# Raw weight slots handed out in order of release, the decay's logarithm issued earlier, and three kinds of attention operations on ScalarE

## The chip, the cores and the metric

The kernel runs on one core of a Trainium2 chip. The metric is the time of one execution on the device in microseconds, the median of several runs; lower is better. The core's engines appear below as PE (TensorE, matrix products), DVE (VectorE), ACT (ScalarE), POOL (GpSimd) and SP (SyncE, which here only issues transfers). Each engine takes its own instructions strictly in order; semaphores make one engine wait for another.

## The reference

One layer with two head groups. 16 learned tokens stand ahead of 512 positions (L = 528), the width is 2048, all in float32:

```python
xn = rmsnorm(h, g_pre)
p = xn @ w_in                       # q, k, v, z_gla, r, hc, gate_b, gate_c, z_conv
log_a = log_sigmoid(r @ w_gate_up + b_gate) / GATE_TAU
o = gla_chunked(q * DK**-0.5, k, v, log_a)      # 4 heads, key 128, value 256, chunks of 64
y_gla = rmsnorm(o, g_gla_out) * silu(z_gla)
y_conv = gate_b * causal_dwconv(gate_c * hc, w_conv) * silu(z_conv)
y = concat([y_gla, y_conv]) @ w_out
return h + rmsnorm(y, g_post)
```

The chunked attention takes the running sum of `log_a` inside a chunk, scales q and k by exponentials of it, forms masked scores, and carries a state of 128 x 256 from chunk to chunk.

## The kernel before

Every float32 product is made of three faster ones. An operand is split into a high half (`whi`, a rounding copy on ACT) and a low half (`wlo`, the raw value minus the high half, on DVE), and PE adds hi*hi, hi*lo and lo*hi.

**Pairs and products.** Two column tiles of the input projection (say `z2` and `z3`) form a `Pair`. A pair is computed by a Strassen-like scheme from its four weight blocks "11", "12", "21", "22" in seven products, in the order P5, P1, P6, P2, P3, P7, P4 (`ORDER`). One product is 24 matmuls of 128 x 128 against about 260 columns. Tile names tell the place: `z2z3P` is the PSUM result of any product of that pair. The third matmul of a product is the first that reads `wlo`. P2 is added into P1's PSUM bank after ACT has copied the bank away (`q`), and P3 into P5's bank after the copy `f`.

**Preparing a product.** `prepare` for a product does up to one add or subtraction of raw blocks on DVE (`raw<-raw`, lines 188 and 218), then the split (`whi` on ACT, line 123, and `wlo` on DVE, line 124). There are three buffers each of `whi` and `wlo`, and products are prepared two ahead of PE (`AHEAD = 2`). `away` takes results out of PSUM, and after each product some steps of the attention generators in `STAGE` run: `decay` (d), `gla_b` (t), `gla_c` (s), `gla_d` (o), `gla_e` (g), one head after the other, from `k1q1` to `b0s0`. A `yield` ends a step.

**Raw slots.** A raw block is 128 x 1024 floats, loaded by one transfer on SP's queue (line 204). Five slots exist, one pool tag with five buffers. Block "21" is last read by the add of P6, "12" by the split of P3, "11" by the split of P7, "22" by the split of P4. `prepare` asks for the next pair's blocks by name at P5, P6 and P4.

**The order.** A scheduler in the framework puts the recorded instructions into one order per engine while the program is built; the places that it chooses are fixed from then on.

**Order of the whole.** First eight plain tiles and the normalisation of x (to about 86 us), then the pairs z2z3, k1q1, v2v3, z4z5, k2q2, v4v5, z6z7, k3q3, v6v7, h0c0, b0s0 with the attention of the four heads between them, then 14 pairs of the convolution, then the output projection and the closing normalisation. `ini` is a pool of the first stage; when it closes, the pools `ev` (the copies `f`, `q`, `u`, `v`) and `gla` take its memory, and a new tile there waits for the last reader of the old tile that lay in the same place.

Of the kernel before, what the change touches and what calls it, by code (L numbers as in the profile page):

```python
# [9 lines left out]
F32 = mybir.dt.float32  # L10
# [35 lines left out]
def hymba_kernel(ctx, tc, xT, x, g_pre, w_r, w_t, w_up, b_gate, g_gla, w_conv, w_o, g_post, out):  # L46
# [29 lines left out]
    wup = const.tile([RU, H * P], F32R, name="wup")  # L76
    bg = const.tile([P, H], F32, name="bg")
    gg = const.tile([P, 2], F32, name="gg")
    wc = const.tile([P, 8, 3], F32, name="wc")
# [39 lines left out]
    def split(raw, shape, pool=None):  # L119
# [5 lines left out]
        return hi, lo  # L125

    def new_raw(shape=None):
        return wp.tile(shape or [P, NB, P], F32, tag="raw", name="raw", bufs=5)

# [12 lines left out]
    def load_gran(name, g):  # L142
        gran = new_gran()
        fill_gran(gran, w_t[TILE[name]], 8 * g, 8 * g + 8)
        return gran

# [43 lines left out]
    class Pair:  # L190
        def __init__(self, na, nb, c0, dst, done=None, stages=(), before=(), per=2):
            self.na, self.nb, self.c0, self.w, self.dst = na, nb, c0, XHALF - c0, dst
            self.done, self.stages, self.before, self.per = done, stages, before, per
            self.raw, self.sb = {}, {}
            for name in ORDER:
                line.append((self, name, name == ORDER[-1]))

        def load(self, b):

            if b not in self.raw:  # L200
                r = new_raw()
                g = NB * (b in ("12", "22"))
                i = TILE[self.na if b[0] == "1" else self.nb]
                nc.sync.dma_start(r, w_t[i][:, g:g + NB, :])
                self.raw[b] = r

        def prepare(self, name, nxt):
            for b in ("21", "22", "11", "12"):
                self.load(b)
            raw = self.raw  # L210
# [10 lines left out]
            two = split(raw[b], [P, NB, P])  # L221
            if nxt and name in ("P5", "P6", "P4"):
                nxt.load({"P5": "21", "P6": "22", "P4": "11"}[name])
                if name == "P4":
                    nxt.load("12")
            return two
# [26 lines left out]
        def away(self, name):  # L253
# [23 lines left out]
            else:  # L277
                self.put(self.dst_b[0], sb["v"], sb["P4"], ALU.subtract)

    def prepare_next():  # L280
        n = len(ready)
        p, name, last = line[n]
        after = [q for q, _, _ in line[n:n + 9] if q is not p]
        ready.append(p.prepare(name, after[0] if after else None))

# [63 lines left out]
    class Whole:  # L349
# [3 lines left out]
        def __init__(self):  # L353
            self.raw, self.pt = {}, None
            for g in range(8):
                line.append((self, g, g == 7))

        def load(self, g):
            g = {"21": 0, "22": 1, "11": 2, "12": 3}.get(g, g)
            if g not in self.raw:  # L360
                r = self.raw[g] = new_raw([P, 2, 2 * OW])
                for c in range(2):
                    nc.sync.dma_start(r[:, :, c * OW:(c + 1) * OW], w_o[c, :, 2 * g:2 * g + 2, :])

        def prepare(self, g, nxt):
            for n in range(min(8, g + 4)):
                self.load(n)
            two = split(self.raw[g], [P, 2, 2 * OW])
            if g < 4:
                self.load(g + 4)  # L370
            else:
                nxt.load(("12", "22", "11", "21")[g - 4])
            return two
# [35 lines left out]
    class Out:  # L409
# [3 lines left out]
        def __init__(self, c, g):  # L413
            self.c, self.g, self.raw = c, g, {}
            self.end = c == 3 and g == 1
            for n in (LORDER if self.end else OORDER):
                line.append((self, n, n == "P4"))

        def load(self, b):
            if b not in self.raw:  # L420
                r = self.raw[b] = new_raw([P, 4, OW])
                k0 = 8 * (b[0] == "2") + 4 * self.g
                nc.sync.dma_start(r, w_o[2 * self.c + (b[1] == "2"), :, k0:k0 + 4, :])

        def prepare(self, name, nxt):
            raw = self.raw
# [9 lines left out]
            two = split(raw[{"P7": "12", "P3": "22", "P2": "21"}.get(name, "11")], [P, 4, OW])  # L436
            if nxt and name in ("P1", "P7", "P3", "P4"):
                nxt.load({"P1": "12", "P7": "22", "P3": "11", "P4": "21"}[name])
            return two
# [181 lines left out]

    with tc.tile_pool(name="ini", bufs=1, reuse_waits="tile") as ini:
        xr = ini.tile([P, KT, L], F32, name="xr")
        rstd = ini.tile([P, L], F32, name="rstd")
# [10 lines left out]
        for n_, (k0, k1) in enumerate(XCUT):  # L635
# [9 lines left out]
            for a, b in WCUT.get(k0, ()):  # L645
                if a == NB:
                    wk[1] = new_gran()
                fill_gran(wk[a // NB], w_t[TILE["k0"]], a, b)
                fill_gran(wq_[a // NB], w_t[TILE["q0"]], a, b)
# [5 lines left out]
            if k0 == 8:  # L655
                nc.sync.dma_start(wup_raw, w_up)
                nc.sync.dma_start(bg, b_gate)
                nc.sync.dma_start(gg, g_gla)
                nc.sync.dma_start(wc, w_conv)
# [6 lines left out]
        for kt in range(KT):  # L666
# [7 lines left out]
            if kt == 10:  # L674
                for n in range(2):
# [4 lines left out]
                    A.activation(rstd[:, t], st_[:, 0:XHALF], AF.Sqrt, bias=epst, scale=1.0 / D)  # L680
                V.reciprocal(rstd, rstd)

        A.copy(wup[0:HI], wup_raw[0:HI])
# [28 lines left out]
        def plain_z(j):  # L712
            if not stage:
                stage.append(new_raw().rearrange("p k c -> p (k c)"))
            zs[j] = stage[0][:, S * j:S * (j + 1)]
            return main_only(zs[j])
# [53 lines left out]
        b11, b12, b21, b22 = B[0, 0], B[0, 1], B[1, 0], B[1, 1]  # L770
        tt = ini.tile([P, NB, XHALF], F32, name="tt")
        do_plain("v0", "v1")
# [11 lines left out]
        do_plain("z1", None)  # L784
        silu(0, 1)
        all_pairs()
        prepare_next()
# [44 lines left out]
    def decay(h):  # L832
# [90 lines left out]
    def gla_c(h):  # L923
# [16 lines left out]
    def gla_d(h):  # L940
# [95 lines left out]
```

## Time and profile before

| | |
|---|---|
| runs | 833.64 us median of 3 (832.9 to 834.14) |
| the profiled execution | 835.32 us; its span from first to last instruction 833.6 us |
| busy PE / DVE / ACT, share of the span | 95% / 84% / 51% |
| mean granted TensorE clock | 0.986 of full speed |
| instructions PE / DVE / ACT | 6364 / 848 / 611 |

The rows further down give a start in us from the span's beginning, a length, the engine, the line of the kernel, and what is written and read. Brackets behind a row hold the idle time of the engine just before it and what released it. The granted clock is 1.00 at full speed (2.4 GHz) and 0.50 at half (1.2 GHz). A wait named for one engine only says which semaphore came last.

### The profile page before, as it was taken

How to read it: one execution, taken by the hardware profiler on the slowest of the kernel's cores; microseconds unless marked ns; L12 is line 12 of the kernel's file. 1: busy time of each engine (PE TensorE's matmuls, PEld its weight loads, DVE VectorE, ACT ScalarE, POOL GpSimd, SP SyncE). 2: the span in 40 equal slices, each digit the busy share in tenths (PEclk: the TensorE clock that was granted, in tenths of full speed). 3: DMA queues.
4: the chain of work that ended last, by engine and by line, in shares of the span. 5: the costliest groups of instructions: out<-in, count | busy, mean ns of one | idle time of the engine just before them, and what ended most of it. 6: DMA issues, size and time to landing. Idle time of an engine off the chain costs nothing.

```text
span 833.6 us, 15174 instructions
## 1 busy us (share of the span) xinstructions
PE 796.1 (95%) x6364; PEld 776.6 (93%) x6364; DVE 699.1 (84%) x848; ACT 428.5 (51%) x611; POOL 2.3 (0%) x14
## 2 busy tenths in 40 slices
PE   8999988999999989999999999999998999999991
PEld 8999888999989989999999999999998889999991
DVE  6999978799798889979888888787879966787887
ACT  7626665485666474544444444444447434444442
POOL 0000000000000000000000000000000000000000
PEclk9999999999999999999999999999998999999996
DMA  9512333234233423263333333333333522333319
GB/s 297 206 54 86 99 118 101 77 117 141 73 101 124 155 77 101 67 213 101 105 110 124 101 116 113 110 109 104 103 101 114 149 92 58 116 99 109 102 59 346
DMA packets 34053, 98.99 MB, mean 119 GB/s; under 512 B 4064, under 2 KB 8800, under 8 KB 33344
## 3 DMA queue, kind: packets, MB, share of 16 engines
q1 hardware_dynamic: 31968, 94.73, 35.2%
q10 hardware_dynamic: 2016, 3.29, 1.3%
q8 instruction: 50, 0.82, 0.4%
q14 instruction: 19, 0.16, 0.1%
HBM read 89.61 MB, written 8.39 MB: 118 GB/s over the span
## 4 chain that ended last, share of the span: by engine, by line
PE 75%; DVE 13%; ACT 4%; DMA 4%; issue 3%; DVEq 0%; SPq 0%; ACTq 0%
PE out L63 5%; PE out1P L63 5%; PE out3P L63 4%; PE out2P L63 4%; DMA raw<-in_w_t_dram 4%; DVE wlo L124 3%; PE v L63 3%; PE v2v3P L63 2%; PE h0c0P L63 2%; PE h6c6P L63 2%; PE h4c4P L63 2%; PE h5c5P L63 2%; PE h3c3P L63 2%; PE h2c2P L63 2%; PE b2s2P L63 2%
## 5 line engine op out<-in xcount | busy, mean ns | idle before, releaser
L123 ACT CAST whi<-raw 128x1024 fp32r<-128x1024 f32 x225 | 235.2, 1050 | 273.2 <-DVE raw L188 91.5
L124 DVE TENSOR_TENSOR wlo<-raw,whi 128x1024 fp32r<-128x1024 f32 x225 | 273.6, 1220 | 62.6 <-ACT whi L123 58.9
L188 DVE TENSOR_TENSOR raw<-raw 128x1024 f32<-128x1024 f32 x75 | 90.3, 1220 | 10.0 <-DMA raw<-in_w_t_dram 9.2
L218 DVE TENSOR_TENSOR raw<-raw 128x1024 f32<-128x1024 f32 x25 | 30.5, 1221 | 0.5
L134 ACT CAST whi<-raw 128x1024 fp32r<-128x1024 f32 (+2 forms) x13 | 10.9, 848 | 20.0 <-PE v L63 12.4
L63 PE MATMUL out<-whi,xt 128*128 128x512 f32 x64 | 20.0, 394 | 0.0
L63 PE MATMUL out2P<-whi,xt 128*128 128x256 f32 x96 | 17.4, 281 | 0.4 <-ACT whi L123 0.4
L63 PE MATMUL out3P<-whi,xt 128*128 128x256 f32 x96 | 17.3, 281 | 0.4 <-ACT whi L123 0.4
L63 PE MATMUL out1P<-whi,xt 128*128 128x256 f32 x96 | 17.3, 281 | 0.0
L63 PEld LDWEIGHTS out2P<-whi,xt 128*128 128x128 f32 x96 | 14.7, 188 | 0.6 <-ACT whi L123 0.6
L63 PEld LDWEIGHTS out3P<-whi,xt 128*128 128x128 f32 x96 | 14.7, 188 | 0.6 <-ACT whi L123 0.6
L63 PEld LDWEIGHTS out1P<-whi,xt 128*128 128x128 f32 x96 | 14.8, 188 | 0.1
L63 PEld LDWEIGHTS out<-whi,xt 128*128 128x128 f32 x64 | 11.9, 188 | 2.7
L63 PE MATMUL out2P<-wlo,xt 128*128 128x256 f32 x48 | 13.5, 280 | 0.0
L63 PE MATMUL out3P<-wlo,xt 128*128 128x256 f32 x48 | 13.5, 280 | 0.0
L63 PE MATMUL out1P<-wlo,xt 128*128 128x256 f32 x48 | 13.4, 280 | 0.0
L135 DVE TENSOR_TENSOR wlo<-raw,whi 128x1024 fp32r<-128x1024 f32 (+2 forms) x13 | 12.5, 968 | 0.6 <-ACT whi L134 0.6
L63 PE MATMUL out<-wlo,xt 128*128 128x512 f32 x32 | 12.6, 394 | 0.0
L577 DVE SCALAR_TENSOR_TENSOR y<-hh,wc,y 128x512 f32<-128x512 f32 x16 | 12.0, 748 | 0.2
L347 ACT ACTIVATE junk<-y 128x256 f32<-128x256 f32 x18 | 7.5, 418 | 8.6 <-DVE y L464 8.4
L63 PE MATMUL out2P<-whi,xa 128*128 128x256 f32 x64 | 11.6, 282 | 0.0
L63 PE MATMUL out3P<-whi,xa 128*128 128x256 f32 x64 | 11.6, 282 | 0.0
(744 smaller groups left out, 2702.0 us busy)
## 6 DMA issues: line engine op xcount, KB each, us to landing
raw<-in_w_t_dram SPq DMA_DIRECT2D x108, 512.0 KB, 4.3
raw<-in_w_o_dram SPq DMA_DIRECT2D x24, 512.0 KB, 4.2
raw<-in_w_o_dram SPq DMA_DIRECT2D x16, 256.0 KB, 3.3
xres<-in_x_dram SPq DMA_DIRECT2D x4, 1024.0 KB, 8.7
xr<-in_xT_dram SPq DMA_DIRECT2D x7, 528.0 KB, 6.4
z<-zd SPq DMA_DIRECT2D x8, 256.0 KB, 2.8
yd<-z SPq DMA_DIRECT2D x8, 256.0 KB, 2.7
yg<-yd SPq DMA_DIRECT2D x1, 2048.0 KB, 10.4
```

Of the source, the lines that this page charges most:

```text
L63: nc.tensor.matmul(out_, lhsT, rhs, start=start, stop=stop, **kw)
L123: A.copy(hi, raw)
L124: V.tensor_tensor(out=lo, in0=raw, in1=hi.bitcast(F32), op=ALU.subtract)
L134: A.copy(hi[:, k, :], raw[:, k, :])
L135: V.tensor_tensor(out=lo[:, k, :], in0=raw[:, k, :], in1=hi[:, k, :].bitcast(F32), op=ALU.subtract)
L188: V.tensor_tensor(out=a, in0=a, in1=b, op=ALU.add)
L218: V.tensor_tensor(out=raw["11"], in0=raw["11"], in1=raw["22"], op=ALU.subtract)
L347: A.activation(junk, oy["src"], AF.Square, accum_out=fin["ssq"][:, t, n:n + 1])
L577: V.scalar_tensor_tensor(out=y, in0=hh[:, i:i + S], scalar=wc[:, j, i:i + 1], in1=y, op0=ALU.mult, op1=ALU.add)
```

## The change

1. **Slots.** The five raw slots become five tags with one buffer each. `free` puts a tag at the end of a list when its last reader has been recorded, and `load_free`, called before and after each `prepare`, gives the first free tag to the next block of one list `loads` for the whole kernel. Where the slot is taken from, and where in the program the load is recorded, is thus decided in the kernel.
2. **Decay.** `min(z + b, 0)` on DVE becomes `relu(-z - b)` on ACT (with `nbg`, the negated bias, made once on POOL). The `Exp` and `Ln` that form the logarithm are recorded a step earlier, and a second `yield` follows them; the subtraction becomes one `scalar_tensor_tensor`.
3. **Attention operations to ACT.** Besides that minimum: the copy of the first state `stt` from PSUM, and the four multiplications per head that normalise the output (`on`).
4. **Memory.** `tt` becomes the first tile of `ini`, ahead of `xr`, so `ev` now lies where `tt` was.

```diff
+    slots = [f"raw{i}" for i in range(5)]
+    held = {}
+
     def new_raw(shape=None):
-        return wp.tile(shape or [P, NB, P], F32, tag="raw", name="raw", bufs=5)
+        tag = slots.pop(0)
+        t = wp.tile(shape or [P, NB, P], F32, tag=tag, name="raw", bufs=1)
+        held[id(t)] = (t, tag)
+        return t
+
+    def free(t):
+        slots.append(held.pop(id(t))[1])
...
+            loads.extend((self, b) for b in self.blocks)
...
+        blocks = ("21", "22", "11", "12")
+
+        def prepare(self, name):
             raw = self.raw
...
-            if nxt and name in ("P5", "P6", "P4"):
-                nxt.load({"P5": "21", "P6": "22", "P4": "11"}[name])
-                if name == "P4":
-                    nxt.load("12")
+            if name in ("P6", "P3", "P7", "P4"):
+                free(raw[{"P6": "21", "P3": "12", "P7": "11", "P4": "22"}[name]])
...
+    loads = []
+
+    def load_free():
+        while slots and loads:
+            p, b = loads.pop(0)
+            p.load(b)
+
     def prepare_next():
-        n = len(ready)
-        p, name, last = line[n]
-        after = [q for q, _, _ in line[n:n + 9] if q is not p]
-        ready.append(p.prepare(name, after[0] if after else None))
+        p, name, last = line[len(ready)]
+        load_free()
+        ready.append(p.prepare(name))
+        load_free()
...
     with tc.tile_pool(name="ini", bufs=1, reuse_waits="tile") as ini:
+        tt = ini.tile([P, NB, XHALF], F32, name="tt")
         xr = ini.tile([P, KT, L], F32, name="xr")
...
             A.activation(a[:, t], zp[:, 0:XHALF], AF.Abs, bias=bg[:, h:h + 1])
-            V.tensor_scalar(out=Bc[:, t], in0=zp[:, 0:XHALF], scalar1=bg[:, h:h + 1],
-                            scalar2=0.0, op0=ALU.add, op1=ALU.min)
-        yield
+            A.activation(Bc[:, t], zp[:, 0:XHALF], AF.Relu, bias=nbg[:, h:h + 1], scale=-1.0)
         A.activation(a, a, AF.Exp, scale=-1.0)
         A.activation(a, a, AF.Ln, bias=1.0)
-        V.tensor_tensor(out=a, in0=Bc, in1=a, op=ALU.subtract)
+        yield
+        yield
+
+        V.scalar_tensor_tensor(out=a, in0=Bc, scalar=-1.0, in1=a, op0=ALU.mult, op1=ALU.subtract)
         V.tensor_tensor_scan(out=Bc, data0=keep, data1=a, initial=0.0, op0=ALU.mult, op1=ALU.add)
...
-        V.tensor_copy(stt[:, 0, :], up[0])
+        A.copy(stt[:, 0, :], up[0])
...
         for p in range(NP):
-            V.tensor_scalar(out=on[:, p, :], in0=o[p], scalar1=ss[:, p:p + 1],
-                            scalar2=None, op0=ALU.mult)
+            A.activation(on[:, p, :], o[p], AF.Copy, scale=ss[:, p:p + 1])
```

`Whole` and `Out`, the classes of the output projection, get the same `free` and one list of loads. In the order that the scheduler makes, nothing differs on any engine behind `b0s0` but line numbers.

How the order moves is seen at three places. The first is SP's queue from the first pair on, where line 204 (216 after) loads raw blocks, line 305 (321) stores a gate tile and line 965 (981) fetches one back. Before:

```order
L204 DMA raw<-in_w_t_dram 128x1024 x2
L305 DMA zd<-raw 128x512
L204 DMA raw<-in_w_t_dram 128x1024 x2
L305 DMA zd<-raw 128x512
L204 DMA raw<-in_w_t_dram 128x1024 x5
L305 DMA zd<-z 128x512
L965 DMA z<-zd 128x512
```

and after:

```order
L216 DMA raw<-in_w_t_dram 128x1024 x4
L321 DMA zd<-raw 128x512
L216 DMA raw<-in_w_t_dram 128x1024
L321 DMA zd<-raw 128x512
L216 DMA raw<-in_w_t_dram 128x1024 x4
L321 DMA zd<-z 128x512
L981 DMA z<-zd 128x512
```

Nine loads stand ahead of the first `z<-zd` in both; two of the first pair and one of the second have moved ahead of a store.

The second place is DVE in k1q1, where the first head's decay runs (`wlo_1339` and `wlo_1380` are the low halves of P2 and P3, the first add is the next pair's). Before:

```order
L188 TENSOR_TENSOR raw_1222<-raw_1222,raw_1291 128x1024
L841 TENSOR_SCALAR B_1320<-zp00_1323,bg_84 128x264
L841 TENSOR_SCALAR B_1320<-zp01_1327,bg_84 128x264
L124 TENSOR_TENSOR wlo_1339<-raw_1190,whi_1338 128x1024
L188 TENSOR_TENSOR raw_1190<-raw_1190,raw_1188 128x1024
L846 TENSOR_TENSOR esx_1321<-B_1320,esx_1321 128x528
L218 TENSOR_TENSOR raw_1188<-raw_1188,raw_1068 128x1024
L847 SCALAR_TENSOR_TENSOR B_1320<-keep_96,esx_1321 128x528
L124 TENSOR_TENSOR wlo_1380<-raw_1190,whi_1379 128x1024
```

and after:

```order
L200 TENSOR_TENSOR raw_1194<-raw_1194,raw_1293 128x1024
L125 TENSOR_TENSOR wlo_1338<-raw_1161,whi_1337 128x1024
L200 TENSOR_TENSOR raw_1161<-raw_1161,raw_1152 128x1024
L229 TENSOR_TENSOR raw_1152<-raw_1152,raw_1070 128x1024
L863 SCALAR_TENSOR_TENSOR esx_1323<-B_1322,esx_1323 128x528
L272 TENSOR_TENSOR u_1409<-k1q1P6_1384,q_1366 128x264
L864 SCALAR_TENSOR_TENSOR B_1322<-keep_97,esx_1323 128x528
L125 TENSOR_TENSOR wlo_1379<-raw_1161,whi_1378 128x1024
```

The two minima are gone, the small subtraction `u` has come ahead of P3's low half, and the scan (`B<-keep,esx`) still stands ahead of it. The decay of the last head, in v6v7, moves in the same way.

The third place is ACT in z4z5, with the second head's decay (`whi_1980` and `whi_2019` are the high halves of P3 and P7). Before:

```order
L261 COPY q_1959<-z4z5P1_1934 128x256
L840 ACTIVATE esx_1969<-zp10_1971,bg_84 128x264
L840 ACTIVATE esx_1969<-zp11_1975,bg_84 128x264
L844 ACT_TABLE_LOAD
L844 ACTIVATE esx_1969<-esx_1969 128x528
L845 ACT_TABLE_LOAD
L845 ACTIVATE esx_1969<-esx_1969 128x528
L123 CAST whi_1980<-raw_1749 128x1024
L123 CAST whi_2019<-raw_1747 128x1024
```

and after, from the normalisation of the head before on:

```order
L973 ACTIVATE on_1788<-o00_1785,ss_1787 128x256 x2
L973 ACTIVATE on_1788<-o01_1786,ss_1787 128x256 x2
L124 CAST whi_1888<-raw_1655 128x1024
L124 CAST whi_1932<-raw_1703 128x1024
L267 COPY f_1919<-z4z5P5_1894 128x256
L270 COPY q_1961<-z4z5P1_1936 128x256
L856 ACTIVATE esx_1971<-zp10_1973,bg_84 128x264
L857 ACTIVATE B_1970<-zp10_1973,nbg_85 128x264
L856 ACTIVATE esx_1971<-zp11_1977,bg_84 128x264
L857 ACTIVATE B_1970<-zp11_1977,nbg_85 128x264
L858 ACT_TABLE_LOAD
L858 ACTIVATE esx_1971<-esx_1971 128x528
L124 CAST whi_1984<-raw_1703 128x1024
L859 ACT_TABLE_LOAD
L859 ACTIVATE esx_1971<-esx_1971 128x528
L124 CAST whi_2020<-raw_1655 128x1024
```

P3's high half (`whi_1984`) now stands between `Exp` and the load of the table for `Ln`, and four `on` and two `relu` have come in. v4v5, with the third head's decay, moves in the same way. Both programs have the same number of table loads on ACT.

## Rows read from the trace of the kernel before

**Rows 1.** Two stretches: busy us of each engine, then granted clock, DMA.

```profile
84.00:385.00 301.00, 286.69 (x2337) 279.80 (x2336) 257.32 (x347) 176.90 (x262) 0.52 (x1) 0.99 0.36 114
385.00:816.00 431.00, 427.03 (x3384) 417.32 (x3383) 353.33 (x380) 200.46 (x277) 0.00 (x0) 0.99 0.34 106
```

**Rows 2.** What PE waited for from 84 to 385 us: total, times, longest.

```profile
PE k1q1P L63 <- DVE wlo L124: 3.5, 3, 2.1
PE v6v7P L63 <- DVE wlo L124: 2.4, 2, 2.1
PE z2z3P L63 <- ACT q L261: 1.9, 1, 1.9
PE v2v3P L63 <- ACT whi L123: 1.6, 1, 1.6
PE z4z5P L63 <- ACT whi L123: 1.6, 1, 1.6
PE v4v5P L63 <- ACT whi L123: 1.6, 1, 1.6
PE b0s0P L63 <- ACT whi L123: 1.0, 1, 1.0
```

**Rows 3.** Groups by line and shape, DVE: busy us, mean ns, idle before.

```profile
L956 DVE TENSOR_SCALAR on<-o,ss 128x256 f32<-128x256 f32 x16 | 6.6, 477 | 0.1
...
L841 DVE TENSOR_SCALAR B<-zp,bg 128x264 f32<-128x264 f32 x8 | 3.5, 482 | 0.0
...
L931 DVE COPY stt<-up 128x256 f32<-128x256 f32 x4 | 1.7, 424 | 1.6 <-PE up L63 1.6
```

**Rows 4.** The same for ACT.

```profile
L951 ACT ACTIVATE on<-o 128x256 f32<-128x256 f32 x16 | 6.0, 380 | 7.0 <-PE o L63 6.7
...
L840 ACT ACTIVATE esx<-zp,bg 128x264 f32<-128x264 f32 x8 | 3.4, 481 | 0.4 <-PE zp L63 0.4
```

**Rows 5.** DVE in order of time, in z2z3.

```profile
79.20 1.26 DVE L756 TENSOR_TENSOR xa<-xr,xa 128x1056 fp32r<-128x1056 f32 x1 [0.47 <-ACT xa L755]
...
98.81 1.22 DVE L124 TENSOR_TENSOR wlo<-raw,whi 128x1024 fp32r<-128x1024 f32 x1
```

**Rows 6.** SP's queue in order of time.

```profile
110.00 1.89 SPq L204 DMA_DIRECT2D raw<-in_w_t_dram  x1
```

**Rows 7.** DVE in order of time, in k1q1 (the first head's decay).

```profile
115.61 1.22 DVE L188 TENSOR_TENSOR raw<-raw 128x1024 f32<-128x1024 f32 x1 [3.81 <-DMA raw<-in_w_t_dram]
116.76 0.88 DVE L841 TENSOR_SCALAR B<-zp,bg 128x264 f32<-128x264 f32 x2
...
122.87 1.20 DVE L124 TENSOR_TENSOR wlo<-raw,whi 128x1024 fp32r<-128x1024 f32 x1
```

**Rows 8.** One stretch: PE busy, granted clock, DMA.

```profile
130.60:134.00 3.40, 3.15 (x14) 0.50 0.51 149
```

**Rows 9.** The chain that ended last: start, us, what.

```profile
130.85 7.03 PE k1q1P L63 x44
...
385.44 19.88 PE b1s1P L63 x168
```

**Rows 10.** ACT in order of time, in z4z5.

```profile
175.05 1.28 ACT L845 ACT_TABLE_LOAD   x1
...
176.90 1.03 ACT L123 CAST whi<-raw 128x1024 fp32r<-128x1024 f32 x1
178.96 1.04 ACT L123 CAST whi<-raw 128x1024 fp32r<-128x1024 f32 x1 [1.03 <-DVE raw L218]
```

**Rows 11.** DVE in order of time, in z4z5.

```profile
178.78 1.22 DVE L124 TENSOR_TENSOR wlo<-raw,whi 128x1024 fp32r<-128x1024 f32 x1
```

**Rows 12.** DVE in order of time, in v6v7 (the last head's decay).

```profile
296.55 1.23 DVE L188 TENSOR_TENSOR raw<-raw 128x1024 f32<-128x1024 f32 x1 [3.26 <-DMA raw<-in_w_t_dram]
...
303.81 1.20 DVE L124 TENSOR_TENSOR wlo<-raw,whi 128x1024 fp32r<-128x1024 f32 x1
```

**Rows 13.** ACT in order of time, in b0s0.

```profile
348.96 0.37 ACT L261 COPY q<-b0s0P 128x256 f32<-128x256 f32 x1
```

More of the change, by code (lines that the diff above doesn't have):

```diff
@@ L77, in hymba_kernel @@
     bg = const.tile([P, H], F32, name="bg")
+    nbg = const.tile([P, H], F32, name="nbg")
     gg = const.tile([P, 2], F32, name="gg")
@@ L144, in load_gran @@
         fill_gran(gran, w_t[TILE[name]], 8 * g, 8 * g + 8)
+        free(gran[2])
         return gran
@@ L196, in __init__ @@
                 line.append((self, name, name == ORDER[-1]))
+            loads.extend((self, b) for b in self.blocks)
         def load(self, b):
[L200 to L209, printed above, removed]
+            r = self.raw[b] = new_raw()
+            g = NB * (b in ("12", "22"))
+            i = TILE[self.na if b[0] == "1" else self.nb]
+            nc.sync.dma_start(r, w_t[i][:, g:g + NB, :])
+        blocks = ("21", "22", "11", "12")
+        def prepare(self, name):
             raw = self.raw
@@ L356, in __init__, with prepare @@
                 line.append((self, g, g == 7))
+                loads.append((self, g))
         def load(self, g):
[L359 to L367, printed above, removed]
+            r = self.raw[g] = new_raw([P, 2, 2 * OW])
+            for c in range(2):
+                nc.sync.dma_start(r[:, :, c * OW:(c + 1) * OW], w_o[c, :, 2 * g:2 * g + 2, :])
+        def prepare(self, g):
             two = split(self.raw[g], [P, 2, 2 * OW])
[L369 to L372, printed above, removed]
+            free(self.raw[g])
             return two
@@ L417, in __init__, with prepare @@
                 line.append((self, n, n == "P4"))
+            loads.extend((self, b) for b in ("11", "12", "22", "21"))
         def load(self, b):
[L420 to L425, printed above, removed]
+            r = self.raw[b] = new_raw([P, 4, OW])
+            k0 = 8 * (b[0] == "2") + 4 * self.g
+            nc.sync.dma_start(r, w_o[2 * self.c + (b[1] == "2"), :, k0:k0 + 4, :])
+        def prepare(self, name):
             raw = self.raw
@@ L436, in prepare @@
             two = split(raw[{"P7": "12", "P3": "22", "P2": "21"}.get(name, "11")], [P, 4, OW])
-            if nxt and name in ("P1", "P7", "P3", "P4"):
-                nxt.load({"P1": "12", "P7": "22", "P3": "11", "P4": "21"}[name])
+            for b in () if self.end else {"P7": ("12",), "P3": ("22",), "P4": ("21", "11")}.get(
+                    name, ()):
+                free(raw[b])
             return two
@@ L646, in hymba_kernel @@
                 if a == NB:
+                    free(wk[0][2])
                     wk[1] = new_gran()
@@ L657, in hymba_kernel @@
                 nc.sync.dma_start(bg, b_gate)
+                G.tensor_scalar(out=nbg, in0=bg, scalar1=-1.0, scalar2=None, op0=ALU.mult)
                 nc.sync.dma_start(gg, g_gla)
@@ L681, in hymba_kernel @@
                 V.reciprocal(rstd, rstd)
+        for raw in (wk[1][2], wq_[0][2], wq_[1][2]):
+            free(raw)
         A.copy(wup[0:HI], wup_raw[0:HI])
@@ L713, in plain_z @@
             if not stage:
-                stage.append(new_raw().rearrange("p k c -> p (k c)"))
-            zs[j] = stage[0][:, S * j:S * (j + 1)]
+                stage.append(new_raw())
+            zs[j] = stage[0].rearrange("p k c -> p (k c)")[:, S * j:S * (j + 1)]
             return main_only(zs[j])
@@ L770, in hymba_kernel @@
         b11, b12, b21, b22 = B[0, 0], B[0, 1], B[1, 0], B[1, 1]
-        tt = ini.tile([P, NB, XHALF], F32, name="tt")
         do_plain("v0", "v1")
@@ L785, in hymba_kernel @@
         silu(0, 1)
+        free(stage[0])
         all_pairs()
```

## The prediction, made before the changed kernel was run

> **What bounds the kernel now.** I read the stretches first. From 385 to 816 us PE is busy for 427.0 of 431 us, and the change moves nothing there or behind; from 84 to 385 us it is busy for 286.7 of 301 us, so 14.3 us of waiting lie where the change works [rows 1]. DVE is busy there for 257 us (85%), ACT for 177 (59%): DVE is the engine with the least to spare. Next, the list of PE's waits: seven rows with 13.6 us, nearly all for a low half from DVE or a high half from ACT [rows 2]. A late half is made late by what stands ahead of it in its engine's queue, so the rest is read in order of time, place by place. Then the clock: from 130.6 to 134.0 us the granted clock is at the lower of its two levels (0.50, 1.2 GHz), right behind the densest group of PE waits, in k1q1 and v2v3 [rows 2, 8]. That costs half of 3.4 us, 1.7 us. Last, the cost of a product: 168 matmuls in 19.88 us are seven products of 2.84 us, 0.118 us a matmul [rows 9].
>
> **The change part by part.**
>
> *Slots: nothing by themselves.* The order of SP's queue shows the same nine loads ahead of the first fetch of z, so the scheduler already handed slots out nearly by release. The three loads that move ahead of a store belong to z2z3 and k1q1, and no PE wait up to 95 us is due to them. Of DVE's two long waits for a block, the first follows a load at 110.00 that must wait for the add of P6 anyway [rows 6, 7], the second likewise [rows 12]. I put slots at 0; the most they could give is those idle times, 3.8 and 3.3 us, the most they could cost is one load that lands late, some 3 us.
>
> *Operations that change engine.* DVE loses 16 `on` at 477 ns, 8 minima at 482 and 4 copies at 424, 13.2 us of busy time [rows 3]. ACT has no row of these forms. From below the nearest is a pass over 128 x 256 of PSUM without a per-partition operand, 380 ns; from above one over 128 x 264 with one, 481 ns [rows 4]. I take 0.48 for `relu` and 0.4 to 0.48 for `on`: about 3.3 us a head, on the engine with room. The page "ScalarE: Activation LUTs" of the Trainium skill (section "Rules for kernel authors") says the opposite of this move: relu, min and mul belong on VectorE, up to about three times faster per element in bf16. For float32 in PSUM the rows do not agree with it, 482 against 481 ns; by the rule the move would only lengthen ACT, and the sum would be that of the second rival below.
>
> Now the places.
>
> *z2z3 (part of A).* P2 waits 1.95 us for `q` on ACT, which stands behind `f`, which waits until DVE is through with blocks of `xr`, because `ev` lies in `xr`'s memory. With `tt` there it needs only `tt`'s last reader, which stands well ahead of those on DVE, so this wait goes. What is late next is P3's low half, on DVE until 100.03 [rows 5]. PE would want that half about 2 us sooner than it did, 2.84 us behind P2's new start, so most of the wait comes back one product later. DVE is 0.47 us ahead, because the first weight add now fills the idle time at 79.2 [rows 5]. I take 0.9 us gained by k1q1, between 0.4 and 1.95.
>
> *k1q1 (A).* The next pair's add waits for its block until 115.61; from there to the end of P3's low half (124.07) DVE works 8.46 us without a pause [rows 7]. After: the minima are gone (0.80 us from start to next start), `u` (0.34) has come in, so 8.0 us. The load follows the add of P6, which PE's pace sets, so the chain starts 0.9 us earlier: P3's low half ends at 115.61 - 0.9 + 8.0 = 122.7, where it was 124.07. PE still waits here, 2.5 to 3 us, because the scan stands ahead of P3's half as before. The wait of P2 ahead of it (0.9) goes. Behind it, before, PE needed 137.88 - 124.07 = 13.8 us to the end of P4 [rows 7, 9]: three products and some transposes are 9.1 us, the rest are waits for `v2v3` (1.65) and P7's low half (0.5), the restarts behind them, and the 1.7 us of slow clock. After, P7 comes in one piece; its low half stands behind five short subtractions and ends about 0.2 us late, P4's behind five multiplications and ends about 0.7 us late. The high half that v2v3 waited for stands behind the exponentials still, but these are some 3 us sooner than PE wants it. So 9.1 + 0.9 = 10.0 us, and P4 ends at 132.7, not 137.88: 5.2 us. I take 5.0. In it is the slow clock: I expect it to stay away, since the waits left behind 116 us are about 3.7 us where the list had 5.1 [rows 2].
>
> *z4z5 and v4v5 (B, C).* Before, P3's high half began at 176.90, behind the load of Ln's table and Ln, and its low half ended at 180.00; P7's high half ended there too [rows 10, 11]. PE wanted them at about 178.4 and waited 1.6 us. After, the high half stands ahead of that load, 1.85 us earlier (176.90 less 175.05), and two relu later (0.9): it ends at about 177.0, the low half at 178.2, in time. P7's high half ends 1.85 + 1.03 us behind P3's, at 179.9, and PE wants it at about 181. The wait goes. What is late next is DVE again. The subtraction of the decay has moved from ahead of P3's half to behind it, so the low halves of the pair that follows come only some 1.2 us sooner while PE comes 1.8 us sooner. I take 1.3 us for each place, between 0.8 and 1.8.
>
> *v6v7 (D).* As in k1q1: the add waits until 296.55 for a block whose load PE's pace sets, and P3's half ends 8.46 us later, at 305.01 [rows 12]; after, 0.46 sooner. P2's wait (0.3) is contained in that. The two loose matmuls each of P7, P4 and h0c0 that PE had begun early and then stood on no longer lie between the products. I take 1.2, between 0.4 and 2.4.
>
> *b0s0.* P3's high half is waited for as before, 1.0 us. New is that `q` (348.96) stands behind four `on` [rows 13], up to 1.9 us later. It is covered: PE has P6 (2.84 us) and eight transposes to do before P2 needs `q`'s bank. Without that cover it costs up to 1.9 us. I take 0. Queued behind the `on` in the other heads are the next high halves; the `on` wait for a reciprocal on DVE, just as they did there, and the halves are prepared two products ahead of PE.
>
> *Sum.* 5.0 + 1.3 + 1.3 + 1.2 = 8.8 us. Against the profiled execution's own time that is 835.32 - 8.8 = 826.5. The median of the runs lies 1.68 us below that execution, so 833.64 - 8.8 = 824.8 us.
>
> **Rivals.**
> *Part of it comes.* The slow clock falls in again behind the remaining wait in k1q1 (1.7 us) and DVE gives only the lower bounds in B, C and D (0.8, 0.8, 0.4): 5.0 - 1.7 + 2.0 = 5.3 us, 828.3. For it: a wait of near 3 us stays just there. Against it: v6v7's wait of 2.1 us by itself was followed by no slow clock.
> *ACT becomes the late engine (slower).* The `on` wait for DVE's reciprocal with the next high halves queued behind them. If all 3.3 us a head reach PE and DVE's relief gains nothing, it is 833.6 + 13.2 = 846.8. It decides when more than 2.2 us a head get through. For it: four of the seven waits are already for ACT [rows 2]. Against it: ACT is idle for 41% of the stretch [rows 1]. The rule cited above speaks for this case.
> *It does nothing.* PE waits for the same chain of DVE by other names, 833.6. For it: the scan still stands ahead of P3's half in k1q1 and v6v7. Against it: z4z5 and v4v5, where a whole table load leaves the way.
> *All waits go.* 14.3 + 1.7 us: 817.6. Against it are the two scans and b0s0.
>
> **Numbers.** Forecast (822 to 827) 0.61, part of it 0.24, all 0.06, nothing 0.05, slower 0.04. The range from 821.5 to 829.8 leaves out the last three and the far ends of the first two. A measurement can tell about 0.2%, 1.7 us, from no change; faster by more 0.91, within it 0.05, slower 0.04.
>
> **What would show it.** PE's idle time from 84 us to the pair h1c1 falls from 14 to about 6 us. No PE wait of over 0.5 us is left in z4z5, v4v5 and v2v3; in k1q1 one of 2 to 3 us for P3's low half stays, in v6v7 one of about 2 us, in b0s0 one of 1 us; in z2z3 the wait is for DVE's low half instead of `q`. The clock is at full speed around 125 to 135 us. DVE's busy time falls by about 13 us, ACT's rises by as much, and everything from h2c2 on takes the same time. Wrong would be: waits for high halves right behind the `on`, a slow stretch anywhere below 385 us, or a load that lands later than before.

## The result, and the profile after

The changed kernel took 828.65 us (median of 4 runs, 827.94 to 829.34) against 833.42 us for the kernel before: a ratio of 0.9942, 95% interval 0.9925 to 0.9959, which is 4.8 us of gain where 8.8 were forecast. A second series of 12 runs gave 828.70 against 831.56 us, 0.9966 (0.9946 to 0.9986), or 2.8 us. It is faster, and inside the range given (821.5 to 829.8), but the forecast of 824.8 us was some 4 us too low; the time lies where the rival "part of it comes" stood (828.3).

The list of PE's waits of the changed kernel, from 84 to 385 us, answers to [rows 2]; the columns are total, times, longest:

```profile
PE k1q1P L63 <- DVE wlo L125: 2.1, 1, 2.1
PE tpm L916 <- DVE vt L260: 1.2, 1, 1.2
PE v6v7P L63 <- DVE wlo L125: 1.2, 1, 1.2
PE z2z3P L63 <- ACT whi L124: 1.0, 1, 1.0
PE b0s0P L63 <- ACT whi L124: 1.0, 1, 1.0
PE k2q2P L63 <- DVE wlo L125: 0.9, 2, 0.5
PE k3q3P L63 <- DVE wlo L125: 0.2, 1, 0.2
```

The waits of z4z5, v4v5 and v2v3 are gone, 1.6 us each (v2v3's was 0.5 us in a second profile of the kernel before). Three new ones stand in the list, `tpm` (in z6z7), k2q2 and k3q3, 2.3 us together, and in z2z3 1.0 us for a high half has taken the place of the wait for `q`. The stretches of [rows 1] again, and a short one at the lower clock, which answers to [rows 8] (PE, PEld, DVE, ACT, POOL busy, granted clock, DMA share, GB/s):

```profile
84.00:385.00 301.00, 293.25 (x2397) 287.09 (x2397) 253.73 (x326) 189.39 (x295) 0.53 (x1) 0.99 0.37 115
385.00:816.00 431.00, 421.41 (x3331) 411.65 (x3329) 353.33 (x385) 198.06 (x276) 0.00 (x0) 0.99 0.35 110
...
123.10:126.50 3.40, 3.40 (x17) 3.40 (x17) 3.40 (x7) 2.68 (x5) 0.00 (x0) 0.50 0.65 161
```

PE is idle for 7.8 us where it was 14.3. The slow clock has not stayed away: it now sits at 123.1 us, right behind k1q1's wait. The operations that changed engine, on ACT, against [rows 3] (busy, mean ns, idle before):

```profile
L973 ACT ACTIVATE on<-o,ss 128x256 f32<-128x256 f32 x16 | 6.2, 471 | 0.0
L857 ACT ACTIVATE B<-zp,nbg 128x264 f32<-128x264 f32 x8 | 3.9, 486 | 0.0
L948 ACT COPY stt<-up 128x256 f32<-128x256 f32 x4 | 1.5, 372 | 0.0
```

471, 486 and 372 ns, where DVE took 477, 482 and 424. The page "ScalarE: Activation LUTs" of the Trainium skill (section "Rules for kernel authors") gives such operations to VectorE, up to about three times faster per element in bf16. In float32 from PSUM these rows show no such difference.

**Sections of the span.** The table was made from the start of each pair's first matmul, in us; "half clock" counts stretches at a granted clock of 0.50 between 84 and 385 us. It also holds the experiments, and a second profile of each kernel (e9, e10).

| profile | z2z3 | k1q1, v2v3 | z4z5, k2q2 | v4v5, z6z7 | k3q3 | v6v7, h0c0 | b0s0, h1c1 | one h pair | half clock |
|---|---|---|---|---|---|---|---|---|---|
| before | 22.10 | 56.77 | 51.77 | 51.80 | 21.23 | 49.26 | 45.89 | 20.03 | 1 |
| before, e9 | 23.61 | 54.10 | 53.03 | 51.80 | 21.23 | 47.83 | 45.21 | 20.03 | 3 |
| e8 shift 32 B | 23.61 | 54.23 | 53.05 | 51.80 | 21.23 | 47.87 | 45.40 | 20.19 | 3 |
| e1 slots alone | 21.35 | 54.09 | 51.83 | 51.80 | 21.22 | 47.83 | 45.67 | 20.03 | 0 |
| after | 21.27 | 52.79 | 51.29 | 51.56 | 22.18 | 47.46 | 45.19 | 20.19 | 1 |
| after, e10 | 21.25 | 53.63 | 51.27 | 51.53 | 21.64 | 49.64 | 45.17 | 20.19 | 2 |
| e4 pad 64 B | 21.25 | 53.28 | 51.29 | 51.58 | 22.33 | 47.47 | 45.05 | 20.03 | 1 |
| e5 tt last | 21.31 | 53.17 | 51.29 | 51.56 | 21.64 | 47.45 | 45.17 | 20.19 | 1 |
| e2 on on DVE | 21.27 | 53.03 | 51.29 | 51.13 | 21.23 | 47.49 | 45.35 | 20.19 | 0 |
| e3 log late | 21.26 | 52.98 | 51.43 | 51.50 | 21.64 | 48.23 | 45.16 | 20.19 | 0 |
| e6 min on DVE | 21.26 | 54.43 | 50.54 | 50.86 | 22.13 | 48.95 | 45.27 | 20.19 | 0 |
| e7 on DVE, pad | 21.28 | 52.72 | 51.27 | 51.09 | 21.25 | 47.46 | 45.78 | 20.03 | 1 |
| e11 mixed | 21.26 | 52.69 | 51.67 | 51.17 | 21.23 | 49.70 | 45.43 | 20.03 | 2 |
| e12 by head | 21.28 | 53.10 | 50.52 | 50.85 | 21.21 | 47.48 | 45.02 | 20.03 | 1 |

Between two profiles of one kernel most sections repeat to 0.05 us where no late load and no stretch at half clock falls in, far better than the times of whole runs do. Three don't: k3q3 took 22.18 and 21.64 us in the changed kernel, which stays unexplained. k1q1 with v2v3, and b0s0 with h1c1, go along with one load each that an add on DVE waits for; the one in k1q1, at the head of the decay's chain, took 4.5 to 5.6 us from issue to add in the 14 profiles.

### The profile page after: what moved, and what is told of

It is laid out like the page before. It is cut to its first block, busy times and chain, and to the rows that moved or that the text cites. A ratio compares the mean times of both kernels' runs of the same rounds, so it can differ in the third digit from the quotient of the medians.

```text
span 826.9 us, 15177 instructions
## 1 busy us (share of the span) xinstructions
PE 796.7 (96%) x6364; PEld 779.1 (94%) x6364; DVE 689.2 (83%) x820; ACT 438.0 (53%) x639; POOL 4.2 (1%) x15
## 4 chain that ended last, share of the span: by engine, by line
PE 80%; DVE 11%; ACT 4%; DMA 3%; issue 2%; SPq 0%; DVEq 0%; ACTq 0%
PE out L63 5%; PE out3P L63 4%; PE out1P L63 4%; PE out2P L63 3%; PE v L63 3%; DVE wlo L125 3%; PE v2v3P L63 2%; PE h0c0P L63 2%; PE h1c1P L63 2%; PE h4c4P L63 2%; PE h6c6P L63 2%; PE h5c5P L63 2%; PE h3c3P L63 2%; PE h2c2P L63 2%; PE b0s0P L63 2%; PE b6s6P L63 2%
## 5 line engine op out<-in xcount | busy, mean ns | idle before, releaser
L63 PE MATMUL out2P<-wlo,xt 128*128 128x256 f32 x48 | 13.5, 281 | 0.0
L63 PE MATMUL out3P<-wlo,xt 128*128 128x256 f32 x48 | 13.5, 281 | 0.0
L63 PE MATMUL out1P<-wlo,xt 128*128 128x256 f32 x48 | 13.5, 281 | 0.0
```

Of the source, the lines that this page charges most:

```text
L63: nc.tensor.matmul(out_, lhsT, rhs, start=start, stop=stop, **kw)
```

## The experiments

Each was timed in one series with the kernel before; ratios have 95% intervals.

**e1, slots alone** (the kernel before with the list of slots, everything else as it was):

```diff
-        return wp.tile(shape or [P, NB, P], F32, tag="raw", name="raw", bufs=5)
+        tag = slots.pop(0)
+        t = wp.tile(shape or [P, NB, P], F32, tag=tag, name="raw", bufs=1)
```

> The kernel before with the raw slots handed out by the list alone; decay, on, stt and tt as before. My account: the scheduler had handed the slots out nearly by release already, so nothing is won, 833.4 us within 1 us, and the same list of PE waits (z4z5 1.6, k1q1 3.0, v6v7 2.1, v4v5 1.5 us) in the trace. Rival: the earlier transfers are part of the gain of 4.8 us; then 829 to 832, and the idle of DVE ahead of the adds at 115.6 and 296.6 us (3.8 and 3.3 us before) is shorter.

830.74 against 832.40 us, 0.9976 (0.9963 to 0.9988): 2.0 us won, not 0. The time is the rival's, but DVE's idle ahead of the two adds is no shorter than in the second profile of the kernel before (2.6 and 1.5 us in both). In the table its own gain is in z2z3, 0.75 us of the 2.0. DVE's rows in order of time show how:

```profile
78.27 1.23 DVE L199 TENSOR_TENSOR raw<-raw 128x1024 f32<-128x1024 f32 x1
79.41 1.26 DVE L769 TENSOR_TENSOR xa<-xr,xa 128x1056 fp32r<-128x1056 f32 x1
```

The first add of weights stands ahead of `xa` instead of behind it and fills the 0.47 us in which DVE waited at 79.2 [rows 5]. The prediction had seen that row move, but put it down to A's 0.9 and not to the slots. The waits of 1.6 us in z4z5, v4v5 and v2v3 are all still in its list of PE's waits, so the slots are not what removed them. The rest by which its trace is shorter (v6v7, k1q1) is the first profile's own, see e9.

**e2, `on` back on DVE** (the changed kernel otherwise):

```diff
-            A.activation(on[:, p, :], o[p], AF.Copy, scale=ss[:, p:p + 1])
+            V.tensor_scalar(out=on[:, p, :], in0=o[p], scalar1=ss[:, p:p + 1],
+                            scalar2=None, op0=ALU.mult)
```

> The changed kernel with the four multiplications of on back on DVE. Account one: after the change PE is waiting for DVE's low halves, so 1.9 us more on DVE per head reaches PE in the pairs behind z4z5, v4v5 and v6v7 by 0.5 to 1.9 us each, hardly in b0s0: 830.2 to 834.4 us, most likely 831.5. Account two: on was off PE's path on either engine, and on ACT it made the transposes ot in k3q3 wait 0.9 us: 827.7 to 828.7 us.

826.66 us, 0.9930 (0.9915 to 0.9945). Account two holds, though the time is 1 us below its range: `on` on ACT wins nothing. That e2 is faster than the changed kernel is not shown by the times, since the intervals overlap. Without it k3q3 takes 21.23 us as before the change, and v4v5 with z6z7 0.4 us less than in the changed kernel. What it does in k3q3 is seen in ACT's rows and in PE's, of the changed kernel, in order of time from the start of that pair:

```profile
262.46 1.28 ACT L970 ACT_TABLE_LOAD   x1
...
265.05 1.05 ACT L124 CAST whi<-raw 128x1024 fp32r<-128x1024 f32 x1 [1.00 <-DVE ss L971]
266.01 1.56 ACT L973 ACTIVATE on<-o,ss 128x256 f32<-128x256 f32 x4
```

```profile
266.56 0.66 PE L986 MATMUL ot<-ident,on 128*128 128x128 f32 x2
267.26 0.33 PE L986 MATMUL ot<-ident,on 128*128 128x128 f32 x1
267.67 0.29 PE L986 MATMUL ot<-ident,on 128*128 128x128 f32 x1
```

PE's transposes of `on` follow ACT's four instructions one by one, from 266.56 to 267.67, because `on` stands behind a high half. The prediction had asked what waits for the next high halves and not who waits for `on` itself.

**e3, the logarithm in its old place:**

```diff
+        yield
         A.activation(a, a, AF.Exp, scale=-1.0)
         A.activation(a, a, AF.Ln, bias=1.0)
-        yield
-        yield
```

> The changed kernel with the exponential and the logarithm of decay issued in their old place, one step later, right ahead of the subtraction and the scan, and without the second yield; relu, on and stt stay on ACT. Account one: the gains inside z4z5 and v4v5 (2.0 and 1.5 us from the start of the pair to its end) come from the high half of P3 no longer standing behind Ln's table; they go, and the waits of near 1.5 us in z4z5 and v4v5 for ACT's high half are back: 830.5 to 832 us. Account two: those gains come from DVE's shorter queue alone and stay: 828 to 829 us.

829.72 us, 0.9965 (0.9948 to 0.9981), between the two accounts. What account one forecast falls: no wait of z4z5 or v4v5 for ACT comes back, and z4z5 with k2q2 stay at 51.43 us. The 0.8 us that it loses stand in v6v7. But the cause that account one gives is not put to the test, because the edit did not bring the high half back behind Ln's table. In the order that the scheduler made, ACT has a high half ahead of each of the two tables in z4z5:

```profile
169.18 1.07 ACT L124 CAST whi<-raw 128x1024 fp32r<-128x1024 f32 x1
170.27 1.28 ACT L859 ACT_TABLE_LOAD   x1
171.56 0.65 ACT L859 ACTIVATE esx<-esx 128x528 f32<-128x528 f32 x1
172.12 1.03 ACT L124 CAST whi<-raw 128x1024 fp32r<-128x1024 f32 x1
173.17 1.28 ACT L860 ACT_TABLE_LOAD   x1
```

**e6, the minima back on DVE**, the logarithm early:

```diff
-            A.activation(Bc[:, t], zp[:, 0:XHALF], AF.Relu, bias=nbg[:, h:h + 1], scale=-1.0)
+            V.tensor_scalar(out=Bc[:, t], in0=zp[:, 0:XHALF], scalar1=bg[:, h:h + 1],
+                            scalar2=0.0, op0=ALU.add, op1=ALU.min)
```

> The changed kernel with the two minima per head back on DVE, and the plain subtraction with them; the logarithm stays early, on and stt on ACT. Account one: it was the minima on DVE (0.8 us per head, ahead of a low half and an add) that made P3's halves late in z4z5 and v4v5; the waits of some 1.6 us there come back, and the low half of P3 in k1q1 ends 0.5 to 1 us later: 830 to 831.7 us. Account two: the logarithm's place removed those waits, which stay away: 828.3 to 829.5 us.

829.69 us, 0.9975 (0.9956 to 0.9993). Its list of PE's waits:

```profile
PE k1q1P L63 <- DVE wlo L125: 2.9, 2, 2.1
PE v6v7P L63 <- DVE wlo L125: 2.1, 1, 2.1
PE v2v3P L63 <- ACT whi L124: 1.6, 1, 1.6
```

Neither account holds whole. The minima make the first head late: v2v3's 1.6 us is back, and k1q1 with v2v3 take 54.43 us, for 53.0 in e2 and e3, where the load in k1q1 was about as late and which, like e6, have no slow stretch there. In v6v7 the wait of 2.1 us for 1.2 shows nothing of the minima: the load there took 5.4 us from issue to add, and with the load in time e1 and e9, with the minima on DVE as well, wait 1.2 us. In z4z5 and v4v5 no long wait came back, and with their successors they even take 0.7 us less each (50.54, 50.86) than in the changed kernel; why is open.

What the profiles with and without the waits of z4z5 and v4v5 differ in is the place of the high half on ACT. In the kernel before (both profiles), e8 and e1 it stands behind both tables (the loads for `Exp` and `Ln`) in both pairs, and PE waits 1.6 us for it in each. In all others but e11 a high half stands ahead of at least one of the two tables, and PE does not wait for ACT there; e11, shown below, has it behind both again. So the prediction's mechanism holds, and either edit without the other let the scheduler move the high half (e3, e6).

**e5, `tt` last again:**

```diff
-        tt = ini.tile([P, NB, XHALF], F32, name="tt")
         xr = ini.tile([P, KT, L], F32, name="xr")
...
         b11, b12, b21, b22 = B[0, 0], B[0, 1], B[1, 0], B[1, 1]
+        tt = ini.tile([P, NB, XHALF], F32, name="tt")
```

> The changed kernel with tt back in its old place, the last tile of ini, so that ev lies over xr again and f must wait for readers of xr. Account one, the prediction's: the gain in z2z3 comes from tt's place; then z2z3 takes 22.1 us again instead of 21.3, with PE waiting 1.9 us for q, and the time is 829.5 us. Account two: the run with the slots alone, where tt also lay last, had z2z3 at 21.35 us; the gain comes from the slots, by way of the first weight add standing earlier on DVE, and z2z3 stays at 21.3 us, the time at 828.7 us.

828.30 us, 0.9957 (0.9940 to 0.9974), and z2z3 at 21.31 us: account two. In its list of PE's waits the one for `q` is there; in the changed kernel's list a wait of 1.0 us for a high half has taken its place, so that `tt`'s move bought nothing:

```profile
PE z2z3P L63 <- ACT q L270: 1.2, 1, 1.2
```

**e4, `nbg` widened to 16 floats**, and **e8, a tile of 4 floats added to the kernel before**:

```diff
-    nbg = const.tile([P, H], F32, name="nbg")
+    nbg = const.tile([P, 16], F32, name="nbg")
```

```diff
     bg = const.tile([P, H], F32, name="bg")
+    nbg = const.tile([P, H], F32, name="nbg")
```

> The changed kernel with the tile nbg widened from 4 to 16 floats per partition, so that all tiles of the left pools lie 64 bytes further than in the kernel before, instead of 32. The order on every engine is that of the changed kernel. Account one: the offset of 32 bytes is what made each h pair from h2c2 on 0.16 us longer (20.19 for 20.03 us) and the output products 0.2 us longer: they go back, 827.5 us. Account two: it is something else, h pairs stay at 20.19 us: 828.7 us.

> The kernel before with a tile of 4 floats per partition added behind bg that nothing reads or writes, so that the tiles of the left pools behind it lie 32 bytes further; the order on every engine is that of before. Account one: the offset alone makes the h pairs slower: 20.19 us for each from h2c2 on instead of 20.03, the time 1 to 1.4 us above before. Account two: the offset does nothing without the change: h pairs at 20.03 us and the time of before, within 0.5 us.

e4: 827.74 us, 0.9939 (0.9921 to 0.9957). e8: 836.30 us, 1.0040 (1.0018 to 1.0062). Four chains that ended last, the first h pair in each: the kernel before, the changed one, e4 and e8.

```profile
405.32 20.03 PE h2c2P L63 x168
```

```profile
398.52 20.19 PE h2c2P L63 x168
```

```profile
399.28 20.03 PE h2c2P L63 x168
```

```profile
403.29 20.19 PE h2c2P L63 x168
```

Account one in both, by the sections: with all later tiles of the left pools 32 bytes further on (by the recorded expectation; the traces hold no addresses), 168 matmuls of 128 x 258 take 0.16 us more, 1 ns each, at a granted clock of 1.00; 64 bytes further they don't. The b pairs (128 x 256) take 19.88 to 19.90 us in all four. From b1s1 to b7s7 that is 0.9 us. The output products out1P and out2P took 39.63 and 40.71 us before, 39.97 and 40.89 us after and in e8, 39.76 and 40.90 in e4: 0.5 us more, of which the pad gives back 0.2. The whole runs show it less well: e8 lost 3.3 us by its ratio, more than these 1.4, and its runs had a mean granted clock of 0.982 for 0.986.

**e9, the kernel before once more, and e10, the changed kernel once more:**

> The kernel before, unchanged, profiled a second time. Account one: the first profile held one-off losses that no change can win back: a load in v6v7 that landed 5.6 us after its issue where five other profiles have 3.7 to 3.9 (1.6 us), a slow clock at 130.6 us (1.7 us) and a second one that was twice as long as in most profiles. Then here v6v7 takes 19.7 us instead of 21.14, the load lands after 3.7 to 4 us, and k1q1 with v2v3 take 54.2 us instead of 56.8; the time is 830 to 833 us. Account two: they belong to the kernel's order; v6v7 takes 21.1 us and k1q1 with v2v3 56.8 us again.

> The changed kernel, unchanged, timed and profiled a second time in one series with the version below. Account one: its gain is that of the first runs, 0.5 to 0.6%, and the version below is 1.5 to 2.5 us faster than this one, as the pairs in its trace are. Rival: the two are the same within 0.5 us, and what the traces give for the two edits is lost again to the clock. In the trace z4z5, v4v5, k2q2 and z6z7 take 21.1, 21.9, 30.2 and 29.6 us, k3q3 22.2 and the h pairs 20.19 us, whatever the clock does.

e9: 834.23 us in its one run, above the range of account one. SP, DVE and PE in v6v7, to be held against [rows 12]:

```profile
290.71 0.33 SPq L204 DMA_DIRECT2D raw<-in_w_t_dram  x1
```

```profile
294.57 1.22 DVE L188 TENSOR_TENSOR raw<-raw 128x1024 f32<-128x1024 f32 x1 [1.50 <-DMA raw<-in_w_t_dram]
```

```profile
303.41 0.39 PE L63 MATMUL v6v7P<-xb,wlo 128*128 128x264 f32 x1 [1.25 <-DVE wlo L124]
```

3.9 us from the issue to the add; in the first profile the same load was issued at 290.94 and the add began at 296.55, 5.6 us. With the load in time PE waits 1.25 us there, as it does after the change. Account one for the load, then, and for k1q1 with v2v3 (54.10 us); the longer stretch at half clock, near 640 us, is as long again (6.8 us in both), so that one is not the first profile's alone. Over all 14 profiles this load took 3.8 to 4.0 us in ten and 5.3 to 5.6 us in four: the first one of the kernel before, e6, e10 and e11. But what the first profile lost there, this one loses elsewhere, to the clock:

```profile
97.10:100.50 3.40, 3.40 (x20) 3.40 (x19) 3.40 (x5) 2.09 (x2) 0.00 (x0) 0.57 0.00 0
124.90:128.30 3.40, 3.40 (x18) 3.40 (x17) 3.30 (x9) 3.24 (x6) 0.00 (x0) 0.50 0.55 154
179.50:182.90 3.40, 3.40 (x19) 3.40 (x18) 3.40 (x8) 2.35 (x4) 0.00 (x0) 0.50 0.79 201
```

Three stretches, each right behind a PE wait, in z2z3, k1q1 and z4z5. The first and the third cost 1.5 and 1.3 us of their sections; the second nothing that shows (54.10 us with it, 54.09 in e1 without one). PE would have waited there anyway: in e1 its waits in k1q1 and v2v3 are 1.6 us longer (2.6 and 1.6 us for 2.1 and 0.5).

e10: 828.70 us as above, a gain of 0.34% where 0.5 to 0.6 was expected; e11, the version of the same series, was 0.55 us faster, close to the rival's 0.5. In its v6v7 the load was late (5.3 us from issue to add) and a half-clock stretch fell in, together 2.2 us. The sections came as expected but for k3q3, 21.64 for 22.2.

**e7, e11, e12: versions.** e7 joins e2 and e4. e11 adds the minima on DVE for heads 1 and 2. e12 has these, the pad, and `on` on DVE for head 2 alone:

```diff
+            if h in (1, 2):
+                V.tensor_scalar(out=Bc[:, t], in0=zp[:, 0:XHALF], scalar1=bg[:, h:h + 1],
+                                scalar2=0.0, op0=ALU.add, op1=ALU.min)
+            else:
                 A.activation(Bc[:, t], zp[:, 0:XHALF], AF.Relu, bias=nbg[:, h:h + 1], scale=-1.0)
...
+            if h == 2:
+                V.tensor_scalar(out=on[:, p, :], in0=o[p], scalar1=ss[:, p:p + 1],
+                                scalar2=None, op0=ALU.mult)
+            else:
                 A.activation(on[:, p, :], o[p], AF.Copy, scale=ss[:, p:p + 1])
```

> The changed kernel with on back on DVE and nbg 16 floats wide, both at once. If the two act in different places, as their traces say (on: the pairs z4z5, z6z7 and k3q3, together 0.8 us; the offset: h pairs and output products, 1.1 to 1.4 us), the gains add up: about 2 us below the changed kernel, 825.5 to 827 us, with h pairs at 20.03 us and k3q3 at 21.2 us. Rival: the run with on back was only a lucky set of clock stretches (8.8 us of slow clock for 10.4), and this one lands at 827.5 to 828.5 us.

> The version with on back on DVE and nbg 64 bytes wide, and further the minimum of heads 1 and 2 back on DVE with the plain subtraction (heads 0 and 3 keep relu on ACT). From the run with all minima on DVE: the pairs k2q2 and z6z7 behind those two heads took 28.75 and 28.93 us instead of 30.18 and 29.63, for 0.7 us lost in z4z5, while heads 0 and 3 lost 2.9 and 1.4 us by it. Account one: relu pays for heads 0 and 3 alone; 1 to 1.5 us below the version without this edit, 824.5 to 825.5 us. Rival: with on on DVE too, DVE is late in z4z5 and v4v5 again, the waits of 1.6 us there come back, and it is 826.5 to 828 us.

> The changed kernel with nbg 64 bytes wide, the minimum of heads 1 and 2 back on DVE with the plain subtraction, and on back on DVE for head 2 alone; all else on ACT as changed. The order on DVE from z4z5 to z6z7 is that of the run with all minima on DVE. Account one, a sum over pairs read from the traces: z4z5 and k2q2 together take 50.5 us (51.3 in the changed kernel), v4v5 and z6z7 50.9 (51.6), k3q3 21.2 (22.2), the h pairs 20.03 each (20.19): 3.5 us less than the changed kernel in all, its mean of 829.1 us becomes 825.6 us. Rival: the pairs do not add up, since each late half starts the next pair's queue anew; then z4z5 with k2q2 and v4v5 with z6z7 stay at 51.3 and 51.6 us, and it is 827 to 828 us.

e7: 825.69 us, 0.9937 (0.9914 to 0.9960), sections as expected. e11: 828.15 us, 0.9953 (0.9935 to 0.9971); the rival: with `on` on DVE too, z4z5's wait is back, for ACT, which now has the high half behind both tables as in the kernel before. In v4v5, where it stands there too, PE waits 0.8 us, for a low half. In its v6v7 the load was late and a slow stretch fell in as in e10. The wait, and ACT's rows ahead of it:

```profile
PE z4z5P L63 <- ACT whi L124: 1.6, 1, 1.6
```

```profile
169.51 1.28 ACT L863 ACT_TABLE_LOAD   x1
170.80 0.65 ACT L863 ACTIVATE esx<-esx 128x528 f32<-128x528 f32 x1
171.35 1.03 ACT L124 CAST whi<-raw 128x1024 fp32r<-128x1024 f32 x1
```

e12: 826.64 us, 0.9925 (0.9907 to 0.9944). All four sections came within 0.05 us of the sums (50.52, 50.85, 21.21, 20.03), so account one, with a mean of 826.3 us where 825.6 was forecast. Its interval lies just below that of e10 (its upper end 0.9944, e10's lower 0.9946; the two series ran on different chips) and overlaps that of the first series; the mean of e10's 12 runs is 829.2 us. The times of the runs don't tell e7 and e12 apart. The sections that the edit touches take 1.0 us less in e12 (0.75 in z4z5 with k2q2, 0.24 in v4v5 with z6z7), and on that ground alone it is the version to take.

## Why the prediction came out too low

The terms, in us; minus is a loss. Both pairs of profiles are read from the table of sections, the last row from the starts of b1s1 and b7s7.

| term | forecast | first profiles | second profiles |
|---|---|---|---|
| z2z3 (A) | 0.9 | 0.83 | 2.36 |
| k1q1 and v2v3 (A) | 4.1 | 3.98 | 0.47 |
| z4z5 with k2q2 (B) | 1.3 | 0.48 | 1.76 |
| v4v5 with z6z7 (C) | 1.3 | 0.24 | 0.27 |
| k3q3 | 0 | -0.95 | -0.41 |
| v6v7 with h0c0 (D) | 1.2 | 1.80 | -1.81 |
| b0s0 and h1c1 | 0 | 0.70 | 0.04 |
| b1s1 to h7c7 | 0 | -0.87 | -0.88 |

**Right:** which waits go (z4z5, v4v5, v2v3) and which stay (k1q1 2.1, b0s0 1.0); that the high half ahead of Ln's table is what takes away the waits of z4z5 and v4v5; the price of `relu` and `on` on ACT; the low half of P3 in k1q1, forecast to end at 122.7, is read by PE at 122.34; and the direction of the busy times (DVE 689.2 us for 699.1, ACT 438.0 for 428.5; 13 were forecast, from mean durations of instructions that overlap). Not as forecast are v6v7's wait, 1.2 us for about 2, and the new one in z2z3, for ACT's high half and not for DVE's low one. The chain of k1q1 stands on DVE as forecast, the scan ahead of P3's half:

```profile
114.17 1.23 DVE L200 TENSOR_TENSOR raw<-raw 128x1024 f32<-128x1024 f32 x1 [2.91 <-DMA raw<-in_w_t_dram]
...
119.93 1.25 DVE L864 TENSOR_TENSOR_SCAN B<-keep,esx 128x528 f32<-128x528 f32 x1
121.09 1.20 DVE L125 TENSOR_TENSOR wlo<-raw,whi 128x1024 fp32r<-128x1024 f32 x1
```

**Wrong in size, B and C (2.6, measured 0.7).** "DVE is late next" was seen, and then priced at 0.3 us a place (1.6 less 1.3). In k2q2 and z6z7 it takes back most of the wait (0.7 us are left in the first profiles; the second ones have a slow stretch in z4z5). PE's rows of the changed kernel, in k2q2 and in z6z7:

```profile
186.40 0.39 PE L63 MATMUL k2q2P<-xa,wlo 128*128 128x264 f32 x1 [0.47 <-DVE wlo L125]
190.91 0.39 PE L63 MATMUL k2q2P<-xt,wlo 128*128 128x264 f32 x1 [0.45 <-DVE wlo L125]
```

```profile
238.80 0.28 PE L916 MATMUL tpm<-ident,vt 128*16 128x128 f32 x1 [1.21 <-DVE vt L260]
```

0.9 of 1.6 us come back in the one and 1.2 of 1.6 in the other. The forecast followed the low halves alone; the second wait is for `vt`, a result taken out of PSUM by the same DVE.

**Wrong step, the slow clock in A (1.7).** "I expect it to stay away" failed: it stands in k1q1 in seven of the ten profiles of the changed kernel and its versions (the changed kernel twice, e4, e5, e7, e11 and e12; not in e2, e3 and e6). It moved from 130.6 us, behind the last of the waits, to right behind P3's wait, and there it costs little. With it, k1q1 with v2v3 take 52.7 to 52.8 us where the load came after 4.5 to 4.6 us, and 53.6 where it took 5.4 (e10); without it 53.0, with loads of 5.4 and 5.5 us (e2, e3). That is 0.6 us at like loads, so this step is not what the sum lacks: A gave 4.8 of its 5.0 us in the first profiles.

**Wrong base, D and k1q1.** [rows 12] and [rows 8] belong to one execution. Its late load (1.6 us) and its stretch at 130.6 us are not the kernel's own: D is worth 0.4 us (47.83 to 47.46) and k1q1 with v2v3 0.5 to 1.3. The forecast then took these losses from a median that already lay 1.68 us below that execution. Execution against execution it was 826.5 us, and 828.88 was measured: 2.4 us too low, where the median came out 3.85 above its forecast.

**Terms put at nothing.** The slots give 0.75 us in z2z3, which the forecast had there for `tt`, so that 0.83 measured for 0.9 is luck; the `on` lose 0.4 to 1.1 in k3q3; and `nbg`, counted as free, costs 1.4 by its size.

**The rival "part of it comes".** Its 828.3 us is met in part by luck. The slow stretch fell in where it said, but A gave 4.8 us in the first profiles where it had 3.3, D 1.8 where it had 0.4, and B and C 0.7 where it had 1.6; k3q3 and the offset, which it did not have, took 2.3 us.

**Where the measured gain came from.** By the sections without a late load or a visible cost of a slow stretch the change wins 0.8 us in z2z3, 0.5 to 1.3 in k1q1 with v2v3, 0.5 in B, 0.2 in C and 0.4 in D, and loses 0.4 to 1.0 in k3q3, 0.9 from b1s1 to b7s7 and 0.5 in the output products: an estimate of 0 to 1.4 us of the 2.8 to 4.8 measured. The rest is argued to be chance and the clock, not shown. The mean granted clock of the runs is 0.986 and 0.985 before (e1's and e10's series) and 0.988 in both series of the changed kernel, but it can't be turned into time directly: in the first profile of the kernel before 13.5 of its 23.7 us at half clock lie behind 820.1 us, where PE has nothing left to do. Ahead of that, half of the time at half clock is 5.1 and 8.5 us in the two profiles before and 3.4 and 5.1 in the two after, at most 1.7 to 3.4 us of gain. That fewer waits leave fewer places for a stretch to follow was only argued, and e1 speaks against it: it has nearly all the waits and no stretch below 385 us. Why e1, e2, e3 and e6 had none stays open. So does the mechanism by which 32 bytes slow a matmul.

## What to carry to other kernels

Price the engine that is late next as carefully as the wait that goes: follow every result that PE reads from it, and take the two pairs as one section. Read the base from two profiles where one can, and mark what only one of them has. Where a scheduler orders the instructions, look up in each version's order where the instruction in question went, since the edit alone doesn't tell. When a small constant is added, look at what its size does to the addresses behind it.

## What was not expected of the hardware

An offset of 32 bytes of the tiles in SBUF made each of six pairs with 258 columns take 20.19 us for 20.03, in both kernels, and left those with 256 columns alone (19.88 to 19.90 us). The same load of 512 KB between the same neighbours took 3.9 us from issue to use in one execution and 5.6 in another. Stretches at half clock fell in other places from one execution of the same kernel to the next (one or three below 385 us), and cost from nothing (k1q1 in e9) to 1.5 us each (z2z3 in e9).
